# Output projection in block order 2, 0, 1, and the first feed-forward product begun with 20 direct tiles, in a hybrid diffusion layer on one core

## The chip, the cores and the metric

The kernel runs on one core of one Trainium2 chip. The metric is the device time of one launch in microseconds (us). A core has TensorE (PE in the profile; its weight loads are listed apart as PEld), VectorE (DVE), ScalarE (ACT), GpSimd (POOL) and SyncE (SP), which here issues nearly all DMA transfers. Each engine works through its own instructions in a fixed order, and an instruction whose operands are not ready holds up all that stand behind it on that engine.

## What is computed

One inference step of a one-layer backbone: 1024 sample tokens and 128 prompt tokens with 1024 features each. What the change touches is the end of the layer, from `merged` on; all of it is fp32.

```
merged = gates[..., :D] * (y_a @ w_proj_a) + gates[..., D:] * (y_b @ w_proj_b)
x = layer_norm(DN_ALPHA * x + gate1 * (merged @ w_out), ln1_g, ln1_b)     # 1024 x 1024
h = x * (1.0 + scale2) + shift2
f = jnp.square(jax.nn.relu(h @ w_ff1)) @ w_ff2                            # 1024 -> 4096 -> 1024
x = layer_norm(DN_ALPHA * x + gate2 * f, ln2_g, ln2_b)
```

Ahead of this stand the adaLN modulation, an input projection, a bidirectional state-space mixer and a gating unit.

## The kernel before

**Tokens and products.** The 1152 tokens are 9 chunks of 128 (chunks 0 to 7 sample, chunk 8 prompt), which make three blocks of 384 tokens: block 0 is chunks 0 to 2, block 1 chunks 3 to 5, block 2 chunks 6 to 8. An fp32 product is made as three fp32r matmuls on operands split in a high and a low part (`mm3`, L89 to L92: hi by hi, hi by lo, lo by hi). `split` (L80) makes the parts: ACT copies the raw tile to hi (L81), then DVE or POOL subtracts, lo = raw - hi (L86).

**Weights.** They come as tiles of 128x1024 (512 KB) through `take`, `more_raw` and `more_split` (L120 to L157): the load is issued on the SP queue (L126) into one of two `w_raw` buffers, and ACT and DVE split it into one of two `w_hi` and two `w_lo` buffers. So a tile can be split only when the tile two places ahead of it has been used up by PE, and loaded only when the tile two ahead has been split (and, in the first feed-forward product, summed).

**Order.** The program is written in one order; the framework's scheduler simulates it and fixes the order of instructions on each engine. `order()` (L113) adds a dependence by hand that carries no wait of its own.

**Output projection** (L876 to L923). For blocks 0, 1, 2 in turn: two halves of 512 output features (`tm_half`, L176), each of four weight tiles; a tile gives 18 matmuls of 512 columns. `ev_o` (L893) evicts the three chunks: DVE multiplies by the gate (L898) and adds the residual (L899). In the second half each chunk goes on at once: DVE statistics and 13 small operations for 1/sqrt by an integer guess and three Newton steps (`ln_stats`), ACT normalises (L904), a DMA stores the chunk to NX, PE transposes it (8 transposes, L912, into two small PSUM buffers), and ACT scales and shifts the result (L916) into `h2f0` or `h2f1` (blocks 0 and 1, fp32) or, for block 2, back in place and then split into `h2h` and `h2l`.

**Operands of the first feed-forward product (FF1)** (`combos`, L862). Blocks 0 and 1 share a Strassen-like scheme on quarters `q11, q21, q12, q22` of their activations: four subtractions of 128x1536 elements (L869 to L872) and seven operands (x11, x21, x22, xt4, xt2, xt3, xt1), each an ACT copy and a DVE subtraction of 128x1536. x11 and x21 are made after block 0, all the rest after block 1.

**FF1** (L978 to L1019). The 32 weight tiles go in 16 pairs. A pair makes seven half products for blocks 0 and 1 (12 matmuls of 384 columns each; four of them with sums of weight quarters, `S`, made by `sums`, L933) and two direct products for block 2 (24 matmuls each): 132 matmuls. `next_pair` takes the next tile after each direct product. Pair 0 has its direct products at the end, because block 2's `h2h` is made last; by hand the transposes of block 2 stand after pair 0's half products (L1008 to L1010). `keep` (L957) makes relu squared (ACT Relu and a DVE square for direct products, L960 and L961; two DVE operations otherwise) and stores it to HID. The second feed-forward product (FF2) follows, reading HID block by block from block 0 on.

Of the kernel before, what the change touches and what calls it, by code (L numbers as in the profile page):

```python
# [12 lines left out]
I32 = mybir.dt.int32  # L13
# [22 lines left out]
def tile_trunk(ctx: ExitStack, tc: tile.TileContext, I, O):  # L36
# [67 lines left out]
    FF0 = len(wsrc)  # L104
    wsrc += [("ff1", I["w_ff1"][i]) for i in range(FT)]
# [26 lines left out]
    def more_split(n):  # L132
        while state["split"] < min(n, len(wsrc)):
# [8 lines left out]
            for cs in cuts_of(i):  # L142
                split(raw[:, cs], hi[:, cs], lo[:, cs], lo_eng["eng"](i))
# [19 lines left out]
    def fm_block(pm, w, act, b, evict):  # L163
# [12 lines left out]
    def tm_half(pm, kind, act_b, evict, early=None):  # L176
        pss = [pm.tile([P, 512], F32, name="mm_ps", tag="mm") for _ in range(3)]
        for kp in range(4):
# [3 lines left out]
            for tt in range(3):  # L182
                for kk in range(2):
# [4 lines left out]
                        k == 0, k == KT - 1)  # L188
# [632 lines left out]
    for ft in range(KT):  # L821
# [12 lines left out]
        add_pos(ft)  # L834
# [20 lines left out]
    X, h_first = {}, {}  # L855

    def operand(name, src):
        t = blk.tile([P, 2, 4, TB], F32R, name=f"x{name}", tag="blk", bufs=NBLK)
        split(src, t[:, 0], t[:, 1], V)
        X[name] = (t[:, 0], t[:, 1])  # L860

    def combos(b):  # L862
        q11, q21, q12, q22 = quad[0, 0], quad[1, 0], quad[0, 1], quad[1, 1]
        if b == 0:
            operand("11", q11)
            operand("21", q21)
            return
        operand("22", q22)
        V.tensor_tensor(q11, q12, q11, op=SUB)  # L869
        V.tensor_tensor(q12, q22, q12, op=SUB)  # L870
        V.tensor_tensor(q22, q22, q11, op=SUB)
        V.tensor_tensor(q21, q22, q21, op=SUB)  # L872
        for name, q in (("t4", q21), ("t2", q22), ("t3", q12), ("t1", q11)):
            operand(name, q)

    for b in range(NB):  # L876
        if b == 2:
            h2b = [blk2.tile([P, KT, TB], F32R, name=f"h2{n}", tag="blk", bufs=NBLK2) for n in ("h", "l")]
        xr = []
        if b == 2:  # L880
            xr2 = blk2.tile([P, 3, D], F32, name="xr2", tag="blk", bufs=NBLK2)

        def load_xr():
            loads = [dma(out=g1[b], in_=GROW[0, b].partition_broadcast(P))] if b < 2 else []
            for c in range(3 * b, 3 * b + 3):
                r = tO.tile([P, D], F32, name="xr", tag="xr", bufs=3) if b < 2 else xr2[:, c % 3, :]
# [5 lines left out]
        for half in range(2):  # L892
            def ev_o(tt, ps):  # L893
                c = 3 * b + tt
                v = 0 if c < NL else 1
                hs = slice(half * 512, (half + 1) * 512)
                t = tO.tile([P, 512], F32, name="ot", tag="ot", bufs=1)
                V.tensor_tensor(t, ps, g1[v][:, hs], op=MUL)  # L898
# [3 lines left out]
                r = xr[tt]  # L902
                mv = ln_stats([r[:, 0:512], r[:, 512:1024]], tO)
                A.activation(r, r, AF.Identity, bias=mv[:, 2:3], scale=mv[:, 1:2])  # L904
                dma(out=NX[c], in_=r)
                for hf in range(2):
                    tp = pxB.tile([P, 4, P], F32, name="h2_ps", tag="aux")
                    ts = slice(tt * P, (tt + 1) * P)
                    ht = r.rearrange("p (k f) -> p k f", f=P)[:, 4 * hf:4 * hf + 4, :] if b == 2 else quad[hf, b][:, :, ts]
                    for a in range(4):  # L910
                        k = hf * 4 + a
                        ins = T.transpose(tp[:, a, :], r[:, k * P:(k + 1) * P], ident)  # L912
                        h_first.setdefault((c, hf), ins)
# [13 lines left out]
    NP = FT // 2  # L927
    S_HOME = [blk if p % 2 else blk2 for p in range(NP - 2)] + [blk, blk2]
    low, high = slice(0, 512), slice(512, D)

    def sums(p):
        r0, r1 = raw_of.pop(FF0 + 2 * p), raw_of.pop(FF0 + 2 * p + 1)
        pl = S_HOME[p]  # L933
        if p == 0:
            ops = [tO.tile([P, 2, 512], F32R, name="S", tag="xr", bufs=3) for _ in range(3)]
        else:
# [306 lines left out]
```

## Time and profile before

| | us |
|---|---|
| median of 3 runs | 1965.96 (1963.28 to 1967.21) |
| profiled execution | 1966.76 |
| its span, first to last instruction | 1965.0 |

| engine | busy us | share of the span |
|---|---|---|
| PE | 1882.0 | 96% |
| DVE | 1244.1 | 63% |
| ACT | 714.0 | 36% |
| POOL | 315.9 | 16% |

A page of the profile gives busy times for the span as a whole; the stretches that the change touches are read from windows, from the waits of PE and from the instructions in order of time. The output projection runs from about 1044 to 1150 us, FF1 from 1150 to 1558 us.

### The profile page before, as it was taken

What the parts mean: (1) busy time and instruction counts of PE and PEld (TensorE: products, weight loads), DVE (VectorE), ACT (ScalarE), POOL (GpSimd) and SP (SyncE); (2) the same over time, 40 slices, a digit from 0 to 9 for tenths busy, and PEclk for the clock granted to TensorE, in tenths of its full rate; (3) what the DMA queues carried; (4) which work ended last, traced back from release to release, by engine and by line L of the source; (5) the groups of instructions that cost most, each with busy time, mean ns of one, the idle gap of its engine ahead of it and who ended that gap; (6) DMA issues with size and microseconds to landing.
All of it is one profiled execution on the core that took longest, in us unless ns stands there. A gap on an engine that the chain in (4) does not pass through costs nothing.

```text
span 1965.0 us, 27909 instructions
## 1 busy us (share of the span) xinstructions
PE 1882.0 (96%) x10555; PEld 1721.4 (88%) x10555; DVE 1244.1 (63%) x2252; ACT 714.0 (36%) x1233; POOL 315.9 (16%) x254
## 2 busy tenths in 40 slices
PE   7999999899999999999999976999999999999998
PEld 4999998787898889999998766999999988878887
DVE  4756857999698353444455785666665555764855
ACT  4443424555413332333332554222222243433431
POOL 0332102333224530155220000000000000000001
PEclk9999999999999999999999987999999999999999
DMA  9145645455575331188545532333334775465551
GB/s 343 57 137 168 203 147 158 135 145 153 191 238 159 125 108 44 33 262 298 152 139 166 179 133 87 118 97 101 98 97 128 269 249 176 171 210 179 174 182 53
DMA packets 139879, 307.58 MB, mean 157 GB/s; under 512 B 14880, under 2 KB 78048, under 8 KB 138592
## 3 DMA queue, kind: packets, MB, share of 16 engines
q1 hardware_dynamic: 139744, 305.80, 47.4%
q8 instruction: 83, 1.36, 0.3%
q14 instruction: 52, 0.43, 0.1%
HBM read 244.23 MB, written 61.51 MB: 156 GB/s over the span
## 4 chain that ended last, share of the span: by engine, by line
PE 77%; DVE 11%; DMA 6%; issue 3%; ACT 2%; POOL 1%; SPq 1%; POOLq 0%; ACTq 0%; DVEq 0%
PE mm_ps L90 18%; PE mm_ps L91 18%; PE mm_ps L92 18%; PE ff_ps L92 6%; PE ff_ps L90 6%; PE ff_ps L91 6%; DVE Fb L584 2%; DVE cbD L587 1%; DVE w_lo L86 1%; DMA w<-in_w_ff_dram 1%; PE s_ps L737 1%; DMA Bb<-FB 1%; PE st_ps L526 1%; DMA xa<-NX 1%; PE y_ps L604 1%
## 5 line engine op out<-in xcount | busy, mean ns | idle before, releaser
L90 PE MATMUL mm_ps<-hTh,w_hi 128*128 128x384 f32 x1032 | 354.7, 347 | 0.8 <-ACT gt L623 0.8
L92 PE MATMUL mm_ps<-hTh,w_lo 128*128 128x384 f32 x1032 | 350.2, 339 | 1.2 <-DVE w_lo L86 1.2
L91 PE MATMUL mm_ps<-hTl,w_hi 128*128 128x384 f32 x1032 | 349.9, 339 | 0.0
L81 ACT ACTIVATE w_hi<-w_raw 128x1024 fp32r<-128x1024 f32 (+1 forms) x143 | 147.7, 1034 | 269.2 <-PE mm_ps L91 101.3
L86 DVE TENSOR_TENSOR w_lo<-w_raw,w_hi 128x1024 fp32r<-128x1024 f32 (+2 forms) x109 | 131.1, 1205 | 165.2 <-ACT w_hi L81 164.6
L90 PE MATMUL ff_ps<-w,hid 128*128 128x512 f32 (+1 forms) x552 | 210.0, 381 | 1.2 <-ACT hid L81 1.2
L91 PE MATMUL ff_ps<-w,hid 128*128 128x512 f32 (+1 forms) x552 | 209.6, 381 | 0.0
L90 PEld LDWEIGHTS mm_ps<-hTh,w_hi 128*128 128x128 f32 x1032 | 195.0, 190 | 11.7 <-issue 7.3
L91 PEld LDWEIGHTS mm_ps<-hTl,w_hi 128*128 128x128 f32 x1032 | 194.4, 188 | 8.9 <-issue 8.3
L92 PEld LDWEIGHTS mm_ps<-hTh,w_lo 128*128 128x128 f32 x1032 | 194.2, 188 | 5.6 <-issue 4.1
L92 PE MATMUL ff_ps<-w,hid 128*128 128x512 f32 (+1 forms) x552 | 170.9, 381 | 1.2 <-DVE hid L86 1.2
L1102 POOL TENSOR_TENSOR xa<-xa,row_lg 128x512 f32<-128x512 f32 (+1 forms) x11 | 15.2, 1396 | 905.2 <-PE ff_ps L92 675.7
L86 DVE TENSOR_TENSOR w<-w,w 128x1024 fp32r<-128x1024 f32 x96 | 117.2, 1222 | 57.9 <-ACT w L81 40.0
L90 PEld LDWEIGHTS ff_ps<-w,hid 128*128 128x128 f32 x552 | 103.8, 188 | 22.8 <-ACT hid L81 2.7
L92 PEld LDWEIGHTS ff_ps<-w,hid 128*128 128x128 f32 x552 | 103.3, 188 | 21.7 <-DVE hid L86 1.7
L91 PEld LDWEIGHTS ff_ps<-w,hid 128*128 128x128 f32 x552 | 103.8, 188 | 19.8
L81 ACT ACTIVATE w<-w 128x1024 fp32r<-128x1024 f32 x96 | 99.3, 1051 | 48.2 <-DMA w<-in_w_ff_dram 43.2
L81 ACT ACTIVATE hid<-hraw 128x384 fp32r<-128x384 f32 x88 | 45.9, 525 | 178.3 <-PE ff_ps L92 172.4
L86 DVE TENSOR_TENSOR hid<-hraw,hid 128x384 fp32r<-128x384 f32 x88 | 49.7, 567 | 82.0 <-ACT hid L81 82.0
L86 POOL TENSOR_TENSOR w_lo<-w_raw,w_hi 128x1024 fp32r<-128x1024 f32 x34 | 84.2, 2476 | 91.9 <-ACT w_hi L81 91.9
L90 PE MATMUL mm_ps<-h2h,w_hi 128*128 128x384 f32 x256 | 86.6, 339 | 3.2 <-ACT h2h L81 3.2
L81 ACT ACTIVATE S<-sum 128x512 fp32r<-128x512 f32 x64 | 39.8, 634 | 129.6 <-DVE sum L943 129.6
(304 smaller groups left out, 4255.2 us busy)
## 6 DMA issues: line engine op xcount, KB each, us to landing
w<-in_w_ff_dram SPq DMA_DIRECT2D x96, 512.0 KB, 5.2
HID<-sq SPq DMA_DIRECT2D x96, 192.0 KB, 2.2
hraw<-HID SPq DMA_DIRECT2D x96, 192.0 KB, 2.8
w_raw<-in_w_ff_dram SPq DMA_DIRECT2D x32, 512.0 KB, 4.0
w_raw<-in_w_v_dram SPq DMA_DIRECT2D x24, 512.0 KB, 3.6
w_raw<-in_w_out_dram SPq DMA_DIRECT2D x24, 512.0 KB, 3.7
Fb<-FB SPq DMA_DIRECT2D x36, 256.0 KB, 4.3
Bb<-FB SPq DMA_DIRECT2D x36, 256.0 KB, 5.1
```

The lines of the kernel that those rows point to most:

```text
L81: A.activation(hi, raw, AF.Copy)
L86: ins = eng.tensor_tensor(lo, raw, hi, op=SUB)
L90: T.matmul(ps, s[0], m[0], start=first, stop=False)
L91: T.matmul(ps, s[0], m[1], start=False, stop=False)
L92: return T.matmul(ps, s[1], m[0], start=False, stop=last)
L526: ins = T.matmul(st, Bk[:, c, g * P:(g + 1) * P], xws[g].rearrange("p h e -> p (h e)"), start=True, stop=True)
L584: V.scalar_tensor_tensor(Fb[:, i, :], Bb[:, i, :], QT[:, c, 3, h:h + 1], Fb[:, i, :], op0=SUB, op1=MIN)
L587: V.scalar_tensor_tensor(cbD[:, i, :], cbL[:, g, :], QT[:, c, 0, h:h + 1], cbD[:, i, :], op0=MUL, op1=ADD)
L604: ins = T.matmul(yp[64 * i:64 * i + 64, q, :], lhs[:, l0 + 64 * j:l0 + 64 * j + 64], rhs[:, j, :], start=n == 0, stop=n == len(terms) - 1)
L737: ins = T.matmul(sps[:, cc, :], Vh[b][:, cc, g * P:(g + 1) * P], WsT[:, g, :], start=True, stop=True)
L1102: mul.tensor_tensor(r[:, s], r[:, s], rows["lg"][:, s], op=MUL)
```

## The change

In the output projection the blocks come in the order 2, 0, 1 (`SEQ`). The layer norm's small operations are made once for the three chunks of a block (`ln_rows`, 128x3 elements) and no longer chunk by chunk. The transposes of a block are put by hand ahead of the first matmuls of the next block's second half (`after` in `tm_half`); those of block 1, which is now last, between the direct products 3 to 6 of FF1. Both gate rows `g1` are loaded with the first block. FF1 begins with 20 direct products for block 2 (tiles 0 to 19). Over those from the sixth on, eleven `tasks` are written one by one: the seven operands and the four subtractions. Then the 16 pairs follow in the order 0, 10, 1, 11, ..., 5, 15, 6, 7, 8, 9; pairs 0 to 9 have seven half products alone (84 matmuls), pairs 10 to 15 keep their two direct products (132). Tiles 0 to 19 are therefore loaded twice, and of ten of them only the upper half is split the second time (`upper`). All squares are made on ACT (Relu, then Square). `S` lies in `blk2` alone, `h2h` and `h2l` in `blk`.

```diff
-    wsrc += [("ff1", I["w_ff1"][i]) for i in range(FT)]
+    ND = 10
+    W_PAIRS = [p for q in range(FT // 2 - ND) for p in (q, ND + q)] + list(range(FT // 2 - ND, ND))
+    wsrc += [("ff1", I["w_ff1"][i]) for i in range(2 * ND)]
+    FF1 = len(wsrc)
+    wsrc += [("ff1", I["w_ff1"][2 * p + j]) for p in W_PAIRS for j in range(2)]
+    upper = {FF1 + 2 * q + 1 for q, p in enumerate(W_PAIRS) if p < ND}
...
-            for cs in cuts_of(i):
+            for cs in [slice(512, D)] if i in upper else cuts_of(i):
...
-                        k == 0, k == KT - 1)
+                        k == 0, k == KT - 1, [after[tt]] if after and k == 0 else ())
...
-        add_pos(ft)
+        add_pos((ft + 6) % KT)
...
-    for b in range(NB):
+    SEQ = (2, 0, 1)
+    for n, b in enumerate(SEQ):
...
-            loads = [dma(out=g1[b], in_=GROW[0, b].partition_broadcast(P))] if b < 2 else []
+            loads = [dma(out=g1[v], in_=GROW[0, v].partition_broadcast(P)) for v in range(2)] if n == 0 else []
...
-                mv = ln_stats([r[:, 0:512], r[:, 512:1024]], tO)
-                A.activation(r, r, AF.Identity, bias=mv[:, 2:3], scale=mv[:, 1:2])
+                V.bn_aggr(mv[:, tt, 0:2], st)
+                if tt < 2:
+                    return
+                ln_rows(mv, 3)
+                for j in range(3):
+                    second(j)
...
-            tm_half(pmB, "out", mp[b], ev_o, load_xr if half == 0 else None)
-        if b < 2:
-            combos(b)
+            tm_half(pmB, "out", mp[b], ev_o, load_xr if half == 0 else None,
+                    [h_last[3 * SEQ[n - 1] + j] for j in range(3)] if n and half else None)
...
+    tasks = deque([lambda: operand("11", q11), lambda: operand("21", q21),
+                   lambda: V.tensor_tensor(q11, q12, q11, op=SUB), lambda: operand("22", q22),
+                   lambda: V.tensor_tensor(q12, q22, q12, op=SUB), lambda: V.tensor_tensor(q22, q22, q11, op=SUB),
+                   lambda: V.tensor_tensor(q21, q22, q21, op=SUB), lambda: operand("t4", q21),
+                   lambda: operand("t2", q22), lambda: operand("t3", q12), lambda: operand("t1", q11)])
...
-        if y is None:
-            A.activation(t, x, AF.Relu)
-            V.tensor_tensor(t, t, t, op=MUL)
-        else:
+        if y is not None:
             V.tensor_tensor(t, x, y, op=op)
-            V.scalar_tensor_tensor(t, t, 0.0, t, op0=MAX, op1=MUL)
+            x = t
+        A.activation(t, x, AF.Relu)
+        A.activation(t, t, AF.Square)
...
+    spare = ["k1", "u2", "u3"]
+    for i in range(2 * ND):
+        done = direct(temp(spare[i % 3]), i, take("ff1"), [h_last[i - 1]] if 4 <= i < 7 else ())
+        if 3 <= i < 6:
+            order(h_first[i], done)
+        if i >= 5 and tasks:
+            tasks.popleft()()
...
-    for p in range(NP):
+    for q, p in enumerate(W_PAIRS):
...
-        if p:
-            direct(p, ft, f0)
-            next_pair(p + 1, 0)
+        if p >= ND:
+            direct(sq(), ft, f0)
+        next_pair(q + 1, 0)
```

What the scheduler makes of it is shown at three places. PE at the start of FF1, before: behind the half products of pair 0 (x22 by the last sum `S4`) stand the transposes of block 2's three chunks, and then the first direct product (`h2h`).

```order
L91 MATMUL mm_ps_10780<-x22_10286,S4_10666 128x384
L92 MATMUL mm_ps_10780<-x22_10286,S4_10666 128x384
L912 MATMUL h2_ps_10543<-ident_77,xr2_10307 128x128 x4
L912 MATMUL h2_ps_10554<-ident_77,xr2_10307 128x128 x4
...
L912 MATMUL h2_ps_10648<-ident_77,xr2_10307 128x128 x4
L90 MATMUL mm_ps_10797<-h2h_10305,w_hi_10494 128x384
L90 MATMUL mm_ps_10832<-h2h_10305,w_hi_10659 128x384
```

After, on PE at the same place, a direct product of block 2 follows the last matmul of the output projection, and the transposes of block 1's first chunk come four direct products later:

```order
L94 MATMUL mm_ps_10351<-w_hi_10400,ml1_8620 128x512
L90 MATMUL mm_ps_10561<-h2h_9594,w_hi_10424 128x384
L93 MATMUL mm_ps_10561<-h2l_9595,w_hi_10424 128x384
L94 MATMUL mm_ps_10561<-h2h_9594,w_lo_10425 128x384
...
L94 MATMUL mm_ps_10666<-h2h_9594,w_lo_10626 128x384
L924 MATMUL h2_ps_10489<-ident_77,xr_10244 128x128 x4
L924 MATMUL h2_ps_10498<-ident_77,xr_10244 128x128 x4
L90 MATMUL mm_ps_10701<-h2h_9594,w_hi_10660 128x384
```

The transposes of the last block no longer stand in one run with PE's next product behind them.

DVE at the making of the activation sums, before (the first rows; `h2f0` and `h2f1` hold blocks 0 and 1, `g1` the gates): they stand between the evictions of block 2, the splits of pair 0's weights and its sums.

```order
L899 SCALAR_TENSOR_TENSOR xr2_10307<-xr2_10307,ot_10416 128x512
L86 TENSOR_TENSOR w_lo_10471<-w_raw_10450,w_hi_10470 128x1024
L869 TENSOR_TENSOR h2f0_9592<-h2f1_9593,h2f0_9592 128x1536
L943 TENSOR_TENSOR sum_10667<-w_raw_10498 128x512
L943 TENSOR_TENSOR sum_10668<-w_raw_10474,w_raw_10498 128x512
L86 TENSOR_TENSOR w_lo_10495<-w_raw_10474,w_hi_10494 128x1024
L898 TENSOR_TENSOR ot_10518<-mm_ps_10419,g1_0_9583 128x512
L870 TENSOR_TENSOR h2f1_9593<-h2f1_9593 128x1536
L86 TENSOR_TENSOR x22_10286<-h2f1_9593,x22_10286 128x1536
```

After, on DVE, they stand between the weight splits of the direct products; `w_lo_10807` belongs to the ninth of them (direct 8, counted from 0), `w_lo_10917` to direct 11:

```order
L86 TENSOR_TENSOR w_lo_10769<-w_raw_10734,w_hi_10768 128x1024
L952 TENSOR_TENSOR h2f0_9592<-h2f1_9593,h2f0_9592 128x1536
L953 TENSOR_TENSOR h2f1_9593<-h2f1_9593 128x1536
L86 TENSOR_TENSOR x22_10876<-h2f1_9593,x22_10876 128x1536
L86 TENSOR_TENSOR w_lo_10807<-w_raw_10772,w_hi_10806 128x1024
...
L86 TENSOR_TENSOR w_lo_10881<-w_raw_10846,w_hi_10880 128x1024
L86 TENSOR_TENSOR xt4_11022<-h2f0_9592,xt4_11022 128x1536
L86 TENSOR_TENSOR xt2_11060<-h2f1_9593,xt2_11060 128x1536
L86 TENSOR_TENSOR xt3_11098<-h2f1_9593,xt3_11098 128x1536
L86 TENSOR_TENSOR xt1_11136<-h2f0_9592,xt1_11136 128x1536
L86 TENSOR_TENSOR w_lo_10917<-w_raw_10884,w_hi_10916 128x1024
```

Written one to a direct product, they have been scheduled in two clusters, ahead of the splits of direct 8 and of direct 11.

ACT at the same four operands, before (`k1` is the eviction of pair 0's first half product):

```order
L81 ACTIVATE w_hi_10659<-w_raw_10498 128x1024
L987 ACTIVATE k1_10696<-mm_ps_10683 128x384
L81 ACTIVATE S_10663<-sum_10667 128x512
L81 ACTIVATE xt4_10293<-h2f0_9592 128x1536
L81 ACTIVATE xt2_10296<-h2f1_9593 128x1536
```

After, on ACT, the four copies stand between Relu (L983) and Square (L984) of direct 8's result `u3_10841`, and the hi part of direct 11's weights behind them:

```order
L81 ACTIVATE w_hi_10880<-w_raw_10846 128x1024
L983 ACTIVATE u3_10841<-mm_ps_10848 128x384
L81 ACTIVATE xt4_11022<-h2f0_9592 128x1536
L81 ACTIVATE xt2_11060<-h2f1_9593 128x1536
L81 ACTIVATE xt3_11098<-h2f1_9593 128x1536
L81 ACTIVATE xt1_11136<-h2f0_9592 128x1536
L984 ACTIVATE u3_10841<-u3_10841 128x384
L81 ACTIVATE w_hi_10916<-w_raw_10884 128x1024
L983 ACTIVATE k1_10879<-mm_ps_10886 128x384
```

The cluster moved from between pair 0's half products to between the direct products of block 2.

## Rows read from the trace of the kernel before

**Rows 1.** PE's waits, 1040 to 1215 us: total, times, longest (us).
```profile
PE mm_ps L90 <- ACT xt L81: 12.1, 3, 10.7
PE h_ps L912 <- ACT xr L904: 6.3, 1, 6.3
PE h_ps L912 <- ACT xr L916: 5.7, 4, 3.8
PE mm_ps L90 <- ACT h2h L81: 3.2, 1, 3.2
PE mm_ps L91 <- DVE w_lo L86: 2.8, 1, 2.8
```

**Rows 2.** Windows: us, PE busy, PEld, DVE, ACT, POOL, PEclk, DMA share, GB/s.
```profile
1160.00:1210.00 50.00, 27.03 (x102) 23.29 (x103) 34.10 (x86) 25.10 (x45) 0.00 (x0) 0.61 0.20 73
...
1300.00:1400.00 100.00, 100.00 (x579) 100.00 (x578) 61.72 (x104) 24.54 (x38) 0.00 (x0) 1.00 0.31 99
```

**Rows 3.** PE over time, start of FF1 to FF2: start, us, line, operation, [idle before].
```profile
1150.16 0.33 PE L90 MATMUL mm_ps<-x,w_hi 128*128 128x384 f32 x1
...
1165.83 0.69 PE L90 MATMUL mm_ps<-xt,w_hi 128*128 128x384 f32 x1 [10.71 <-ACT xt L81]
...
1170.26 0.52 PE L92 MATMUL mm_ps<-xt,w_lo 128*128 128x384 f32 x1
...
1175.65 0.33 PE L92 MATMUL mm_ps<-xt,S 128*128 128x384 f32 x1
...
1204.30 1.01 PE L90 MATMUL mm_ps<-h2h,w_hi 128*128 128x384 f32 x2 [3.23 <-ACT h2h L81]
...
1558.48 0.39 PE L90 MATMUL ff_ps<-w,hid 128*128 128x512 f32 x1
```

**Rows 4.** PE over time, a stall in block 2's output projection.
```profile
1119.35 0.50 PE L91 MATMUL mm_ps<-w_lo,mh 128*128 128x512 f32 x1 [2.75 <-DVE w_lo L86]
1119.69 0.40 PE L92 MATMUL mm_ps<-w_hi,ml 128*128 128x512 f32 x1
```

**Rows 5.** DVE over time: block 0's first eviction, and ahead of that stall.
```profile
1074.59 0.68 DVE L898 TENSOR_TENSOR ot<-mm_ps,g 128x512 f32<-128x512 f32 x1
...
1113.55 1.75 DVE L86 TENSOR_TENSOR x<-h2f,x 128x1536 fp32r<-128x1536 f32 x1
...
1116.41 1.75 DVE L86 TENSOR_TENSOR x<-h2f,x 128x1536 fp32r<-128x1536 f32 x1
1118.08 1.22 DVE L86 TENSOR_TENSOR w_lo<-w_raw,w_hi 128x1024 fp32r<-128x1024 f32 x1
```

**Rows 6.** ACT over time in the output projection: weight splits, normalising, evictions, operands.
```profile
1051.95 1.06 ACT L81 ACTIVATE w_hi<-w_raw 128x1024 fp32r<-128x1024 f32 x1 [3.02 <-PE mm_ps L92]
1057.36 1.06 ACT L81 ACTIVATE w_hi<-w_raw 128x1024 fp32r<-128x1024 f32 x1 [4.34 <-DMA w_raw<-in_w_out_dram]
...
1087.81 1.24 ACT L904 ACTIVATE xr<-xr,ln_mv 128x1024 f32<-128x1024 f32 x1 [2.15 <-DVE ln_mv L213]
...
1100.21 2.91 ACT L916 ACTIVATE h2f<-h_ps,H,S 128x128 f32<-128x128 f32 x8 [1.42 <-PE h_ps L912]
...
1110.32 2.90 ACT L81 ACTIVATE x<-h2f 128x1536 fp32r<-128x1536 f32 x2
```

**Rows 7.** Window around the late weight tile (columns as in rows 2).
```profile
1051.00:1056.00 5.00, 5.00 (x24) 4.14 (x23) 1.23 (x1) 1.06 (x1) 0.00 (x0) 1.00 1.02 401
```

**Rows 8.** PE over time: one chunk's eight transposes at full clock.
```profile
1092.56 1.04 PE L912 MATMUL h_ps<-ident,xr 128*128 128x128 f32 x8
```

**Rows 9.** Groups by line and shape, 1210 to 1550 us: busy us, mean ns, idle before.
```profile
L86 DVE TENSOR_TENSOR w_lo<-w_raw,w_hi 128x1024 fp32r<-128x1024 f32 x30 | 36.8, 1226 | 94.5 <-ACT w_hi L81 94.5
...
L961 DVE TENSOR_TENSOR sq<-sq 128x384 f32<-128x384 f32 x31 | 17.1, 552 | 0.0
L960 ACT ACTIVATE sq<-mm_ps 128x384 f32<-128x384 f32 x31 | 14.6, 472 | 0.0
```

**Rows 10.** The page's DMA issues: count, KB each, us to landing.
```profile
w_raw<-in_w_ff_dram SPq DMA_DIRECT2D x32, 512.0 KB, 4.0
```

More of the change, by code (lines that the diff above doesn't have):

```diff
@@ L87, in split, with mm3 @@
         return ins
-    def mm3(ps, s, m, first, last):
-        T.matmul(ps, s[0], m[0], start=first, stop=False)
+    def mm3(ps, s, m, first, last, after=()):
+        ins = T.matmul(ps, s[0], m[0], start=first, stop=False)
+        for a in after:
+            order(ins, a)
         T.matmul(ps, s[0], m[1], start=False, stop=False)
@@ L854, in tile_trunk @@
     quad = {(r, b): h2f[b][:, 4 * r:4 * r + 4, :] for r in range(2) for b in range(2)}
[L855 to L874, printed above, removed]
@@ L876, in tile_trunk, with ln_rows @@
-    for b in range(NB):
-        if b == 2:
-            h2b = [blk2.tile([P, KT, TB], F32R, name=f"h2{n}", tag="blk", bufs=NBLK2) for n in ("h", "l")]
+    h2b = [block(blk, F32R, f"h2{n}", NBLK) for n in ("h", "l")]
+    X, h_first, h_last = {}, {}, {}
+    def ln_rows(mv, n):
+        x = mv[:, :, 1]
+        V.tensor_scalar(x, x, EPS, None, op0=ADD)
+        y = tO.tile([P, n], F32, name="ln_y", tag="ln_y", bufs=2)
+        t = tO.tile([P, n], F32, name="ln_t", tag="ln_t", bufs=2)
+        V.tensor_scalar(y.bitcast(I32), x.bitcast(I32), 1, None, op0=ALU.logical_shift_right)
+        V.tensor_scalar(y.bitcast(I32), y.bitcast(I32), -1, 0x5F3759DF, op0=MUL, op1=ADD)
+        for it in range(3):
+            V.tensor_tensor(t, y, x, op=MUL)
+            V.tensor_tensor(t, t, y, op=MUL)
+            V.tensor_scalar(t, t, -0.5, 1.5, op0=MUL, op1=ADD)
+            V.tensor_tensor(x if it == 2 else y, y, t, op=MUL)
+        V.scalar_tensor_tensor(mv[:, :, 2], mv[:, :, 0], -1.0, x, op0=MUL, op1=MUL)
@@ L901, in ev_o, with second @@
                     return
-                r = xr[tt]
-                mv = ln_stats([r[:, 0:512], r[:, 512:1024]], tO)
-                A.activation(r, r, AF.Identity, bias=mv[:, 2:3], scale=mv[:, 1:2])
+                st = tO.tile([P, 2, 6], F32, name="ln_st", tag="ln_st", bufs=2)
+                for i in range(2):
+                    V.bn_stats(st[:, i, :], xr[tt][:, i * 512:(i + 1) * 512])
+                V.bn_aggr(mv[:, tt, 0:2], st)
[4 more added lines that the diff above has]
+                    second(j)
+            def second(j):
+                c = 3 * b + j
+                v = 0 if c < NL else 1
+                r = xr[j]
+                A.activation(r, r, AF.Identity, bias=mv[:, j, 2:3], scale=mv[:, j, 1:2])
                 dma(out=NX[c], in_=r)
@@ L984, in tile_trunk @@
         ft = 2 * p
[L985 removed]
         k1, u2, u3 = temp("k1"), temp("u2"), temp("u3")
+        p1 = half_product(f0, "11")
         A.activation(k1, p1, AF.Copy)
[L988 to L997 removed]
+        p2 = half_product(f0, "21", high)
+        keep(sq(), ft, 0, p2, k1)
+        if p >= ND:
+            direct(sq(), ft, f0)
+        next_pair(q + 1, 0)
+        p4 = half_product(f1, "t4", high)
+        if p >= ND:
+            direct(sq(), ft + 1, f1)
+        next_pair(q + 1, 1)
+        p6 = half_product(s2, "t2")
         V.tensor_tensor(u2, p6, k1, op=ADD)
[L999 removed]
+        p7 = half_product(s3, "t3")
         V.tensor_tensor(u3, p7, u2, op=ADD)
[L1001 to L1003 removed]
+        keep(sq(), ft + 1, 0, u3, p4, SUB)
+        p5 = half_product(s1, "t1")
+        keep(sq(), ft + 1, 1, p5, u3)
         V.tensor_tensor(u2, p5, u2, op=ADD)
[L1005 to L1018 removed]
+        p3 = half_product(s4, "22")
+        keep(sq(), ft, 1, p3, u2)
     stV.close()
```

94 lines of the change are left out of this document (36 added, 58 removed).

## The prediction

> **What bounds the kernel now.** I read the waits of PE around the end of the output projection first, then the windows, then PE, DVE and ACT in order of time. In the windows of FF1 from 1210 us on, PE is busy without a break: 100.00 of 100 us, 579 matmuls, granted clock 1.00, so one matmul of 384 columns comes every 100 / 579 = 0.173 us [rows 2]. There is nothing to gain there. The start of FF1 is different. Between 1160 and 1210 us PE is busy 27.03 of 50 us, at a granted clock of 0.61 on average [rows 2], and PE's waits name the reasons in the order of the work [rows 1]: 12.1 us for operands xt on ACT (10.7 in one piece), 6.3 for the normalising of block 2, 5.7 for the evictions that free its two transpose buffers, 3.2 for h2h. Over time [rows 3]: PE stops ahead of 1165.83 because the four operands wait for the DVE subtractions; it starts again at the lower of its two clock levels (1.2 against 2.4 GHz; 17 matmuls from 1170.26 to 1175.65, 0.317 us each), and the same follows the wait that ends at 1204.30. A stall of 2.75 us at 1119.35 has another cause: two operand subtractions (DVE, 1.75 us each) stand ahead of the weights' lo part [rows 4, 5]. After that one the next matmul comes 0.34 us later and runs 0.40 us, near the full rate [rows 4]: a stall of this length did not take the clock down, one of 10.71 us did.
>
> **What the change removes.** FF1 lasts from 1150.16 to 1558.48 us [rows 3], 408.3 us. Its matmuls are 16 x 132 = 2112, before and after. At 0.173 us they take 365.4. Of the other 42.9 us, the 24 transposes of the last block are work that stays in this stretch: three times 1.04 [rows 8] = 3.1. So 39.8 us are waits and slow clock. All of them come from one thing: FF1's first pair needs sums over blocks 0 and 1, and its direct products need block 2, both of which are made at that moment. After the change, the first 20 tiles' direct products need only block 2, which was finished a whole block earlier, and take 20 x 24 x 0.173 = 83 us; the normalising of block 1 and the operands are made meanwhile. The two operands no longer stand together ahead of one weight split, so the 2.75 us of the present stall go as well; what one of them costs at its new place is in (c). Removed: 39.8 + 2.75 = 42.6 us.
>
> **What it adds, on the path.** (a) *The second gate row.* It is loaded with the first block, 512 KB more ahead of that block's next weight tile. That tile is already the late one: its hi part starts at 1057.36, 5.41 us after the one at 1051.95, where a tile's 18 matmuls of 512 columns take 18 x 0.173 x 512 / 384 = 4.15, and it waits for its DMA [rows 6], while the queues move 401 GB/s at a share of 1.02 [rows 7]. PE is still busy throughout [rows 7], but little can be left over. 524 KB at 401 GB/s is 1.3 us; bounds 0 (it finds room) and 2; I take 1.2.
>
> (b, c) *Transposes inside the next block's second half.* For the blocks 2 and 0 they now stand by hand ahead of the first products of the three chunks, and each chunk's eight evictions (2.91 us [rows 6]) stand on ACT ahead of a weight tile's hi part (1.06), which DVE's lo part (1.23 [rows 9]) follows: 5.2 us in a row where a tile lasts 4.15. With block 2, copies to h2h stand among them; with block 0, the operand x11, one half of the 2.90 us of two [rows 6], and its DVE part of 1.75 [rows 5]. In the present order the same row of work cost PE nothing at 1100.21, so the bounds of each are 0 and three times 1.1; since more is packed in, I take the upper end less a little, 3 us for each of the two halves, 6 in all.
>
> (d) *The two clusters in the direct products.* A direct product lasts 24 x 0.173 = 4.16 us. Block 1's last chunk is transposed behind direct 5; its evictions end about 1.04 + 2.91 = 3.95 us into direct 6. Only then can DVE make two subtractions and x22's lo part, which start 1.67 us apart [rows 5], and behind them stands direct 8's weight lo part, ready 3.95 + 5.0 + 1.2 = 10.15 us after direct 6 began; direct 8 wants it at 8.5. That is a wait of 1.65. Ahead of direct 11 stand four operands: after direct 8's Relu four ACT copies of 1.4, and four DVE subtractions of 1.67, the first of which can start 2.9 us into direct 9; direct 11's lo part is ready at 2.9 + 6.7 + 1.2 = 10.8 against 8.5, a wait of 2.3, less some 0.4 since the matmuls with hi alone are put ahead. With 0.25 us for the two transpose buffers, (d) is 1.65 + 1.9 + 0.25 = 3.8; bounds 0 (the subtractions find gaps that I don't see) and 8 (each cluster costs twice as much).
>
> (e) *What lies beside other work.* Ten more splits of whole tiles and ten of upper halves (ACT 1.06, DVE 1.23 for a whole one), and 20 more loads of 512 KB. In a direct product ACT has 1.06 + 2 x 0.47 [rows 6, 9], DVE 1.23, of 4.16 us. In a pair of half products alone (84 x 0.173 = 14.5 us) DVE has two splits, four sums with their lo parts and the combinations, some 11 us by the same rows, ACT less. So neither is the bound; I cost them at 0, and if the cover failed a pair would be late by what DVE exceeds 14.5, on ten pairs at most 10 us in all. The 96 squares taken off DVE (552 ns each [rows 9]) cost and gain nothing where PE waits for no one. In the clusters of (d) they would stand ahead of the late splits.
>
> The Trainium skill (ScalarE: Activation LUTs, Rules for kernel authors) speaks against this last part: Relu, maxima and products belong on VectorE rather than ScalarE. The rows say otherwise for this form: ACT's Relu over 128x384 took 472 ns, DVE's square 552 ns [rows 9]. Going by the page, the squares would stay on DVE, each of the two waits of (d) would be up to 0.55 us longer, and the time 1936; going by the rows it is 1935.
>
> **The sum.** 42.6 removed; 1.2 + 6 + 3.8 = 11.0 added. The profiled execution took 1966.76 us, so 1966.76 - 31.6 = 1935.2; the median of the runs is 0.8 lower, which I leave out. Forecast 1935, with its own range from 1928 to 1942 by the bounds that can fall together.
>
> **Rivals.** *No new waits.* Each of (a) to (d) comes out near its lower end: 1966.8 - 42.6 = 1924. For it speaks that the chain of evictions and splits cost PE nothing at 1100.21; against it the stall at 1119.35, which is the same thing as the two clusters [rows 4, 5].
>
> *The old waits come back in another place.* Block 1's normalising has to be ready when its transposes' turn comes, four direct products (16.6 us) after FF1 begins. Block 0's first normalising began 13.2 us after its first eviction (1074.59 to 1087.81 [rows 5, 6]) and takes 1.24, and now it waits for all three chunks' statistics; some 2 us are left over. If they aren't there, PE waits behind direct 3 for the normalising and then for the buffers, at most as now 6.3 + 5.7 [rows 1], and restarts at the low clock, which costs 17 x (0.317 - 0.173) = 2.4 [rows 3]: 1935.2 + 14.4 = 1950. The change would do half of what it says.
>
> *Slower than before: direct products that aren't fed.* The place is the two raw buffers during the first 20 tiles. A buffer's round is its load (4.0 us [rows 10]), then ACT 1.06 and DVE 1.23, 6.3 us, and two direct products give it 8.3. It decides when the landing grows past 6.0 us; beyond that each tile is late by half of the excess, and to eat the 31.6 us over 20 tiles takes 3.2 us of excess, a landing of 9.2. At 10 us it would be (10 + 2.3 - 8.3) / 2 x 20 = 40 us, 1975. Against it: the output projection's tiles are as short (4.15 us), and one tile was late there, while 2 MB were loaded beside it [rows 6, 7].
>
> **How the numbers follow.** Forecast 0.56, no new waits 0.20, old waits 0.17, unfed 0.04; the remaining 0.03 is a mixture of the last two that ends within 0.2% (about 4 us, what a measurement of this kernel can tell from no change). Faster 0.93, same 0.03, slower 0.04. The range for 8 in 10 is 1922 to 1950: from no new waits, less 2 for the estimate of the rate, up to the waits that come back.
>
> **What would show it.** In the changed profile: FF1's first matmul is a direct product within a microsecond of the last one of the output projection; from there to FF2's first matmul it takes some 372 us (365.4 + 3.1 + 3.8) and the granted clock stays 1.00; PE's waits name w_lo or w_hi at directs 8 and 11 with 1 to 3 us; the output projection from first to last matmul is some 4 us longer than now (7.2 added, 2.75 gone), with waits for w_lo, w_hi or the transpose buffers in the second halves of blocks 0 and 1; the pairs show none. Wrong would be: a wait for the normalising behind direct 3, waits for w_raw's DMA in the directs, or a granted clock under 1 in them; and waits in the short pairs for S or w_lo, which I cost at nothing.

## The result and the profile after

The changed kernel takes 1937.0 us (median of four runs, 1936.3 to 1941.1) against 1965.3 before: ratio 0.986, 95% interval 0.9843 to 0.9878. The forecast was 1935. The profiled execution has a span of 1935.2 us.

The time is best followed in four stretches: up to the first matmul of the output projection, from there to the first matmul of the first feed-forward product (FF1), from there to the first of the second (FF2), and to the end. All four borders are rows of PE in order of time.

| us | ahead | output projection | FF1 | FF2 and end | span |
|---|---|---|---|---|---|
| before | 1043.6 | 106.6 | 408.3 | 406.5 | 1965.0 |
| after | 1040.4 | 114.8 | 373.3 | 406.6 | 1935.2 |
| difference | -3.1 | +8.2 | -35.0 | +0.1 | -29.8 |

The first column can't be told from scatter. Ahead of the output projection the change moves only the order of `add_pos`; the eleven variants below, which all have that and alter nothing more there, lie between 1038.8 and 1044.4. So in the trace the change gives 26.6 us, from the output projection on, and that sum (span less the first column; before 921.4, after 894.8) is what the traces of the experiments are compared by.

The waits of PE from the output projection to the end of FF1, in the changed kernel (us in total, times, longest), answer to rows 1:

```profile
PE mm_ps L90 <- ACT w_hi L81: 6.6, 5, 2.1
PE mm_ps L93 <- DVE w_lo L86: 1.6, 3, 1.0
PE mm_ps L94 <- DVE w_lo L86: 0.5, 1, 0.5
PE h_ps L924 <- ACT h2f L929: 0.3, 1, 0.3
PE h_ps L924 <- ACT xr L929: 0.3, 1, 0.3
```

No wait for an operand xt, for the normalising or for h2h is left (L929 is the eviction of a transposed chunk); 8.7 of the 9.3 us that remain are for weight splits. Where they lie, PE in order of time (start, us, line, operation, idle before; L90, L93 and L94 are the three matmuls of a product):

```profile
1058.44 0.96 PE L90 MATMUL mm_ps<-w_hi,mh 128*128 128x512 f32 x3 [1.48 <-ACT w_hi L81]
1059.70 0.50 PE L93 MATMUL mm_ps<-w_lo,mh 128*128 128x512 f32 x1 [0.30 <-DVE w_lo L86]
...
1060.42 0.63 PE L90 MATMUL mm_ps<-w_hi,mh 128*128 128x512 f32 x1
...
1106.73 0.96 PE L90 MATMUL mm_ps<-w_hi,mh 128*128 128x512 f32 x3 [1.35 <-ACT w_hi L81]
...
1145.67 0.96 PE L90 MATMUL mm_ps<-w_hi,mh 128*128 128x512 f32 x3 [2.14 <-ACT w_hi L81]
1147.65 0.50 PE L93 MATMUL mm_ps<-w_lo,mh 128*128 128x512 f32 x1 [1.02 <-DVE w_lo L86]
1147.99 0.39 PE L94 MATMUL mm_ps<-w_hi,ml 128*128 128x512 f32 x1
...
1155.27 0.33 PE L90 MATMUL mm_ps<-h2h,w_hi 128*128 128x384 f32 x1
...
1205.09 0.44 PE L90 MATMUL mm_ps<-h2h,w_hi 128*128 128x384 f32 x1 [0.88 <-ACT w_hi L81]
...
1206.42 0.44 PE L90 MATMUL mm_ps<-h2h,w_hi 128*128 128x384 f32 x1 [0.70 <-ACT w_hi L81]
...
1207.55 0.69 PE L94 MATMUL mm_ps<-h2h,w_lo 128*128 128x384 f32 x1 [0.49 <-DVE w_lo L86]
...
1528.55 0.39 PE L90 MATMUL ff_ps<-w,hid 128*128 128x512 f32 x1
```

There are four places: the first tile of block 2's second half (1058), the second half of block 0 (1107), that of block 1 (1146), and directs 11 and 12 (1205). Behind the first and the last, matmuls of 0.63 and 0.69 us show the lower clock.

A stop costs more than the wait that is listed for it: the three matmuls at 1145.67 took 1.98 us to the next one at 1147.65, where the full pace (0.227 us each) makes 0.68, so 1.30 were lost where the list has 1.02. Counted like this, from start to start and with the slow matmuls, the changed kernel lost 3.9 us at 1058, 3.0 in block 0's second half, 4.2 in block 1's, and 4.2 at directs 11 and 12: 15.3 in all.

In windows (us, PE busy, PEld, DVE, ACT, POOL, PEclk, DMA share, GB/s) the stretch of rows 2 that had a granted clock of 0.61 now has 0.97, and the pairs are as full as they were:

```profile
1160.00:1210.00 50.00, 47.92 (x274) 46.51 (x273) 32.77 (x41) 38.37 (x65) 0.00 (x0) 0.97 0.54 178
1230.00:1330.00 100.00, 100.00 (x579) 100.00 (x578) 62.57 (x95) 54.41 (x98) 0.00 (x0) 1.00 0.40 131
```

What makes directs 11 and 12 late stands on ACT in order of time: four copies as one piece between the weight splits.

```profile
1196.75 1.06 ACT L81 ACTIVATE w_hi<-w_raw 128x1024 fp32r<-128x1024 f32 x1 [3.44 <-DMA w_raw<-in_w_ff_dram]
1197.71 0.48 ACT L983 ACTIVATE u<-mm_ps 128x384 f32<-128x384 f32 x1
1198.08 5.61 ACT L81 ACTIVATE xt<-h2f 128x1536 fp32r<-128x1536 f32 x4
1203.59 0.51 ACT L984 ACTIVATE u<-u 128x384 f32<-128x384 f32 x1
1204.00 1.04 ACT L81 ACTIVATE w_hi<-w_raw 128x1024 fp32r<-128x1024 f32 x1
```

### The profile page after: what moved, and what is told of

The parts are those of the page before. It is cut to its first block, busy times and chain, and to the rows that moved or that the text cites. A ratio compares the mean times of both kernels' runs of the same rounds, so it can differ in the third digit from the quotient of the medians.

```text
span 1935.2 us, 27993 instructions
## 1 busy us (share of the span) xinstructions
PE 1876.0 (97%) x10555; PEld 1715.9 (89%) x10555; DVE 1214.2 (63%) x2107; ACT 802.2 (41%) x1413; POOL 317.1 (16%) x254
## 4 chain that ended last, share of the span: by engine, by line
PE 76%; DVE 11%; DMA 6%; ACT 3%; issue 3%; POOL 1%; SPq 0%; POOLq 0%; ACTq 0%; DVEq 0%
PE mm_ps L93 18%; PE mm_ps L94 18%; PE mm_ps L90 17%; PE ff_ps L94 6%; PE ff_ps L90 6%; PE ff_ps L93 6%; DVE Fb L590 1%; DVE w_lo L86 1%; PE y_ps L610 1%; DVE cbD L593 1%; DVE X L671 1%; DVE crow L250 1%; PE s_ps L743 1%; DMA ada_b<-in_w_ada_dram 1%; PE st_ps L532 1%
## 5 line engine op out<-in xcount | busy, mean ns | idle before, releaser
L90 PE MATMUL mm_ps<-hTh,w_hi 128*128 128x384 f32 x1032 | 354.0, 347 | 0.7 <-ACT gt L629 0.7
L94 PE MATMUL mm_ps<-hTh,w_lo 128*128 128x384 f32 x1032 | 350.1, 339 | 0.0
L93 PE MATMUL mm_ps<-hTl,w_hi 128*128 128x384 f32 x1032 | 349.9, 339 | 0.0
L81 ACT ACTIVATE w_hi<-w_raw 128x1024 fp32r<-128x1024 f32 (+2 forms) x163 | 164.5, 1011 | 263.1 <-PE mm_ps L93 136.0
L86 DVE TENSOR_TENSOR w_lo<-w_raw,w_hi 128x1024 fp32r<-128x1024 f32 (+2 forms) x129 | 150.0, 1165 | 147.8 <-ACT w_hi L81 147.2
L90 PE MATMUL ff_ps<-w,hid 128*128 128x512 f32 (+1 forms) x552 | 209.8, 381 | 1.8 <-ACT hid L81 1.8
L93 PE MATMUL ff_ps<-w,hid 128*128 128x512 f32 (+1 forms) x552 | 209.6, 380 | 0.0
L90 PEld LDWEIGHTS mm_ps<-hTh,w_hi 128*128 128x128 f32 x1032 | 194.3, 189 | 11.0 <-issue 7.3
L93 PEld LDWEIGHTS mm_ps<-hTl,w_hi 128*128 128x128 f32 x1032 | 194.4, 188 | 8.9 <-issue 7.0
L94 PEld LDWEIGHTS mm_ps<-hTh,w_lo 128*128 128x128 f32 x1032 | 194.2, 188 | 4.3 <-issue 4.3
L94 PE MATMUL ff_ps<-w,hid 128*128 128x512 f32 (+1 forms) x552 | 171.1, 380 | 1.0 <-DVE hid L86 1.0
L1121 POOL TENSOR_TENSOR xa<-xa,row_lg 128x512 f32<-128x512 f32 (+1 forms) x11 | 15.3, 1404 | 877.8 <-ACT xa L1120 877.8
L90 PEld LDWEIGHTS ff_ps<-w,hid 128*128 128x128 f32 x552 | 103.8, 188 | 22.6 <-ACT hid L81 2.8
L94 PEld LDWEIGHTS ff_ps<-w,hid 128*128 128x128 f32 x552 | 103.3, 188 | 21.3 <-DVE hid L86 1.4
L93 PEld LDWEIGHTS ff_ps<-w,hid 128*128 128x128 f32 x552 | 103.8, 188 | 19.8
L90 PE MATMUL mm_ps<-h2h,w_hi 128*128 128x384 f32 x256 | 86.6, 338 | 1.6 <-ACT w_hi L81 1.6
L94 PE MATMUL mm_ps<-h2h,w_lo 128*128 128x384 f32 x256 | 86.3, 338 | 0.5 <-DVE w_lo L86 0.5
```

Source lines behind the costliest of these rows:

```text
L81: A.activation(hi, raw, AF.Copy)
L86: ins = eng.tensor_tensor(lo, raw, hi, op=SUB)
L90: ins = T.matmul(ps, s[0], m[0], start=first, stop=False)
```

## The experiments

The theory: FF1's gain comes from work that stands beside the 20 directs (the normalising and transposes of block 1, and the sums), and the losses are weight splits that come late for three separate reasons: one late load, and two rows of work ahead of the splits on ACT and DVE. The rivals: the gain comes from the block order, the batched layer norm or the squares; the losses are a general lack of room on ACT, DVE or the queues. All variants start from the changed kernel.

**e10: the sums behind the directs.** Each part is also held behind the last weight split, as in e3 below.

```diff
-        if i >= 5 and tasks:
-            tasks.popleft()()
+        while i == 2 * ND - 1 and tasks:
+            made = tasks.popleft()()
...
```

> The operands and subtractions are all held back by hand to the end of the direct products (behind the split of the first pair's first tile), so that the directs cover the layer norm of block 1 and its transposes, but not the sums. Theory (what the directs hide is the waits that pair 0 had before the change: 10.7, 0.7, 0.7, 0.5 us and some 4 us of slow matmuls behind them, some 16 us): these come back ahead of pair 0, less the 4.2 us at 1205 us and some 2 us at 1146 that go: 1937 + 10 = 1947, between 1943 and 1955. Rival (the gain comes from the block order, the batched layer norm and the squares, and the place of the sums matters little): 1931 to 1938.

Measured: 1946.7 us (1943.8 to 1948.2). From the output projection on 901.6 us, FF1 385.7 against 373.3. PE's waits in FF1 are the old ones of rows 1, at the new place:

```profile
PE mm_ps L90 <- ACT xt L81: 12.6, 2, 11.9
PE mm_ps L93 <- DVE x L86: 0.6, 1, 0.6
```

So hiding the sums beside the directs is worth about what they cost ahead of pair 0. The normalising and its transposes, still covered here, do not come back as waits. Some 18 us against the kernel before remain without the sums' share; no run here tells the block order from the directs in them, since the directs need block 2 to be finished first.

**e3: the sums truly one to a direct.** Each operand's ACT copy and each DVE part is held behind the split of the weight tile last written (dependences on the same engine); in e2 only x11 and x21 are held.

```diff
...
-            tasks.popleft()()
+            made = tasks.popleft()()
+            if 1 <= 11 - len(tasks) <= 11:
+                hi, lo = made if type(made) is tuple else (None, made)
+                order(lo, state["w_lo"])
+                if hi is not None:
+                    order(hi, state["w_hi"])
```

> All eleven operands and subtractions are held back by hand, one behind the weight split of each direct from the fifth on, on ACT and on DVE, so that the clusters ahead of directs 8 and 11 are gone. Theory (the cluster of four costs the waits and the slow clock around 1205 us, about 4.2 us, and x11 and x21 those of 3.2 at 1146): 1937.0 - 7.4 = 1929.6 if nothing comes back, 1932 with half of x11's and x21's share back. Rival (ACT and DVE have too little room in the directs however it is spread): waits of 1 to 2 us at several directs, 1935 to 1940.

> The operands x11 and x21 are held back by hand to directs 5 and 6 (each behind the split of the next tile), where the program has them; in the changed kernel the scheduler puts them into the last half of the output projection. Theory (they are what makes the last weight tiles of the output projection late): the waits of 2.14 and 1.02 us at 1146 us go, 3.2 us. In directs 4 to 7 ACT then has 1.06 + 1.0 + 2.9 + 1.5 = 6.4 us for 4.16 at two tiles, so that up to 3 of it can come back there: 1934 to 1937, 1935 if half comes back. Rival (the weights are late there because of the evictions alone): no change, 1937.

Measured: e3 1929.3 us (1928.0 to 1932.8), ratio to before 0.9827 (0.9808 to 0.9845). FF1 takes 369.5 us, which is the 365.4 of its matmuls, the 3.1 of its transposes and 1 us; its only wait is

```profile
PE h_ps L925 <- ACT h2f L930: 0.4, 1, 0.4
```

and the window of the directs runs at full clock:

```profile
1152.00:1252.00 100.00, 99.56 (x584) 99.22 (x583) 63.95 (x79) 67.62 (x108) 0.00 (x0) 1.00 0.55 177
```

There was room enough on ACT and DVE (68 and 64 of 100 us busy); the cluster was the cost. e2 came out at 1937.7 (1933.3 to 1940.1); its trace, of the fastest of its runs, gives 892.7, 2.1 below the changed kernel. The pair of waits at 1146 shrank from 2.14 and 1.02 to 0.77 and 0.30, not to nothing, while FF1 became 2.3 longer behind the cluster that stayed. So x11 and x21 are only part of what stands ahead of the last tiles. In both traces the output projection is 4.6 us shorter, but only some 2.1 of that lies at 1146; the rest lies at 1058, which neither edit touches: the waits there are 0.24 and 0.28 in e2, 0.45 and 0.29 in e3, and the clock did not fall behind them.

**e8: the transposes of blocks 2 and 0 where the scheduler puts them.**

```diff
             tm_half(pmB, "out", mp[b], ev_o, load_xr if half == 0 else None,
-                    [h_last[3 * SEQ[n - 1] + j] for j in range(3)] if n and half else None)
+                    None)
```

> The transposes of blocks 2 and 0 are not put by hand ahead of the first products of the next block's second half; the scheduler places them. In its order each group of four or eight evictions has a weight split between, where the changed kernel has 24 and 20 evictions in a row around one or two. Theory (these groups make the next weight tile late): the waits at 1107 us (1.35 + 0.30) and about 1 us of those at 1146 go, but x11 and x21 now stand together ahead of the third direct product's split and cost 1 to 2 there: 1934 to 1937. Rival (the scheduler puts the transposes where PE would wait for their operands): waits for xr or h_ps, 1938 to 1942.

Measured: 1929.1 us (1927.6 to 1931.2), ratio 0.9827 (0.9812 to 0.9841), more than expected. The output projection takes 104.9 us against 114.8. From 1060 us to its end one wait is left:

```profile
PE mm_ps L93 <- DVE w_lo L86: 0.3, 1, 0.3
```

It belongs to the place at 1058. The hand-made order of the transposes caused all of the waits in the second halves of blocks 0 and 1. Of the 9.9 us, counted from start to start, 7.2 lie in these two halves; the other 2.7 lie at 1058, which this edit does not touch (waits of 0.54 and 0.29 here, and no slow matmuls). FF1 is 2.0 us longer (375.3): x11 and x21 now make the third direct's split late, as expected (a wait of 0.62 at 1156), and one of 0.66 for the transposes' buffers at 1171 comes to it.

**e1: the first block's loads in three pieces.**

```diff
...
-            loads = [dma(out=g1[v], in_=GROW[0, v].partition_broadcast(P)) for v in range(2)] if n == 0 else []
-            for c in range(3 * b, 3 * b + 3):
+            loads = [dma(out=g1[kp], in_=GROW[0, kp].partition_broadcast(P))] if n == 0 and kp < 2 else []
+            for c in [3 * b + kp] if n == 0 else range(3 * b, 3 * b + 3):
```

> The loads ahead of block 2 (two gate rows and three residual chunks, 2.5 MB, issued in one piece behind one weight tile in the changed kernel) are issued in three pieces behind three weight tiles. Theory (the second gate row makes a weight tile late): the waits of 1.48 and 0.30 us at 1058 us and the slow matmuls behind them (about 1.6 us) go, 1937.0 - 3.4 = 1933.6. Rival (the sum of the bytes in that stretch is what delays, wherever they are issued): another tile is late by as much, 1936 to 1938.

Measured: 1936.7 us (1935.6 to 1938.3), by the time of the launch no change. The trace says otherwise: the only wait between 1044 and 1100 us is

```profile
PE h_ps L926 <- ACT xr L931: 0.3, 1, 0.3
```

so the late tile is gone, and with it the 3.9 us of this place. The output projection is only 2.1 us shorter, because slow matmuls followed the unchanged waits of block 1's half (from 1148.74 on), where the changed kernel had none. From the output projection on the sum is 891.0, 3.8 less; the other 1.6 lies in FF1, which the edit does not touch: this time the clock did not fall behind directs 11 and 12. This execution began the output projection at 1044.4, the latest of all, which hides it in the total. The gain is shown for this place and trace, not for the launch.

**e4 and e12: squares on DVE, in the changed kernel and in the best one.**

```diff
-        if y is not None:
-            V.tensor_tensor(t, x, y, op=op)
-            x = t
-        A.activation(t, x, AF.Relu)
-        A.activation(t, t, AF.Square)
+        if y is None:
+            A.activation(t, x, AF.Relu)
+            V.tensor_tensor(t, t, t, op=MUL)
+        else:
+            V.tensor_tensor(t, x, y, op=op)
+            V.scalar_tensor_tensor(t, t, 0.0, t, op0=MAX, op1=MUL)
```

> Squares as before the change (DVE, ACT only Relu for direct products); all else as changed. Theory (neither engine holds up PE in the pairs, and the squares cost or gain nothing): 1937 to 1938, the waits around 1205 us up to 0.5 longer, none in the pairs. Rival (the squares' move is what gives DVE room in the pairs without direct products): DVE has four more operations of 0.55 in pairs of 14.5 us; waits for w_lo or S in ten pairs, 1942 to 1947.

> e9 with the squares on DVE as before the change. Theory (the 4 us that the squares on DVE cost in e4 came only through the cluster at 1205 us and through restarts at the low clock, and DVE has room everywhere else): the same as e9 within 2 us, 1920 to 1924. Rival (the squares on ACT are worth 4 us on their own, in the pairs and at the start of FF2): 1925 or more, with waits for w_lo or S in the pairs or a longer wait at the start of FF2.

Measured: e4 1941.4 us (1938.7 to 1941.9), 4 more than the changed kernel and more than the theory allowed; e12 1923.1 against e9's 1922.4 (below), no difference. In e4 there is no wait in the pairs; the waits at directs 11 and 12 became 1.28, 0.72 and 0.90 instead of 0.88, 0.70 and 0.49, and FF1 2.4 us longer, with some 16 slow matmuls behind them in place of 8. The output projection is 1.6 longer with the same waits, at a granted clock of 0.94 from 1095 to 1150 us where the changed kernel had 1.00; that has nothing to do with squares. FF2 is 2.1 longer, some 0.4 of it a longer wait at its start. With the clusters gone, e12 has no wait at all from the first matmul of the output projection to the end of FF1, and the difference is gone too. So the pairs have room for the squares on either engine; what they cost in e4 they cost at the clusters, as far as it is not scatter.

**e6 and e13: how many directs are needed.** e6 changes the changed kernel (`ND = 5`, ten directs), e13 the best one (`ND = 8`, 16 directs).

> Ten direct products ahead of the pairs in place of 20, and ten tiles loaded twice in place of 20 (pairs 0 to 4 without direct products, 5 to 15 with). The last operand is ready 51 us after the first direct product began in the changed kernel (1206.3 less 1155.3), ten directs with three times eight transposes last 45 us, and pair 0's sums and splits now stand between the operands on DVE. Theory (20 directs are more than needed, ten are too few): pair 0 waits 4 to 8 us in pieces, with 2.4 us of slow matmuls: 1944, between 1940 and 1949. Rival (pair 0's first products need only x11 and x21, which are ready, and hide the rest): 1934 to 1938.

> e9 with 16 direct products first in place of 20, four tiles fewer loaded twice, and pairs in the order 0, 8, 9, 1, 10, 11, 2, 12, 13, 3, 14, 15, 4 to 7. Theory (the cover is needed only until the last operand is made, one per direct from the fifth to the fifteenth): the same as e9 within 1.5 us, 1920 to 1923. Rival (16 are just too few, since x and xt end with the last direct and pair 0 needs its sums from the same engine): a wait of 2 to 5 us ahead of pair 0, 1924 to 1927.

Measured: e6 1938.2 us, but between 1934.5 and 1947.4; e13 1922.6 (1919.6 to 1927.9), the same as with 20. e6's profiled execution is its slowest run. Its waits in FF1 are two:

```profile
PE mm_ps L94 <- DVE w_lo L86: 2.5, 1, 2.5
PE mm_ps L90 <- ACT w_hi L81: 1.3, 1, 1.3
```

That is 3.8 us where 4 to 8 were expected, FF1 is 2.7 us longer than with 20 directs, and the median lies below the 1940 to 1949 expected. My expectation counted the operands as if pair 0 wanted them all at once; it wants them over 14.5 us, which I take to be the reason. Against the trace of the changed kernel this slowest execution loses 3.8 us ahead of the output projection (1044.3), 2.9 in it (117.7, with nearly the same waits, but low clock behind those at 1111 and 1153, where the changed kernel kept the full one), 2.7 in FF1 and 0.9 in FF2. Its faster siblings left no trace. Ten directs are nearly enough, 16 are enough; the exact need stays open within the scatter.

**e7: the layer norm chunk by chunk.**

```diff
-                if tt < 2:
-                    return
-                ln_rows(mv, 3)
-                for j in range(3):
-                    second(j)
+                ln_rows(mv[:, tt:tt + 1, :], 1)
+                second(tt)
```

> The layer norm's small operations chunk by chunk (three times 14 operations of 128x1 in place of 14 of 128x3), and each chunk normalised when its own are done; all else as changed. Theory (DVE has room in that stretch, and the turn of the transposes is set by hand): no change, 1936 to 1939. Rival (the batch is what lets the last block be normalised before direct 4): a wait for xr on PE behind direct 3 of 2 to 5 us, 1939 to 1945.

Measured: 1938.4 us (1936.0 to 1940.4). PE waits 1.87 us for xr at 1101 in block 0's half and not behind direct 3; its output projection is 3.4 us longer than the changed kernel's, its FF1 1.8 shorter. The batch is worth no more than the measurement can tell.

**e9: e1, e3 and e8 together.**

> Three of the edits together: the first block's loads in three pieces (e1), the operands and subtractions held to one per direct product (e3), and the transposes of blocks 2 and 0 left to the scheduler (e8). Theory (the new waits of the change have three separate causes, each of which one edit removes): from the first matmul of the output projection the changed kernel took 894.8 us to the end, e3 885.3, e8 886.2; e8's output projection less the 0.8 us at 1059 is 104.1, e3's FF1 369.5, FF2 405.6, together 879: 1937 - 16 = 1921, between 1919 and 1925. Rival (the slots in the directs are full, and what e8 spreads in the output projection collides with what e3 holds back): waits in directs 2 to 8 of 2 to 5 us, 1924 to 1929.

Measured: 1922.4 us (1920.4 to 1924.1), ratio to before 0.9786 (0.9773 to 0.98). From the output projection on 879.6, 15.2 below the changed kernel: that is what the four places cost there from start to start (15.3). The windows of the output projection and of FF1, and all of PE's waits in them:

```profile
1041.00:1144.00 103.00, 103.00 (x478) 85.38 (x478) 69.07 (x122) 50.43 (x80) 0.00 (x0) 1.00 0.61 207
1144.00:1513.00 369.00, 368.56 (x2137) 368.21 (x2135) 224.64 (x334) 208.30 (x365) 0.00 (x0) 1.00 0.46 151
```

```profile
PE h_ps L927 <- ACT h2f L932: 0.4, 1, 0.4
```

But for this wait, PE works without a break at full clock over 472 us. This version beats both kernels.

## Why the prediction came out right, point by point

**What is removed** (42.6 us): right. The 39.8 us of FF1 were waits and slow clock and nothing else: with the collisions gone (e3, e9) FF1 takes 369.5 us where the prediction's floor was 365.4 + 3.1, and e9 against the kernel before is 41.8 us from the output projection on. e10 shows for the sums' share that their place among the directs is what does it, and e7 and e12 that the batched norm and the squares are not. That the waits for the normalising, the buffers and h2h went because of the directs is read from the trace alone, which has none of them left. The 2.75 us of rows 4 did go.

**(a) The second gate row** (1.2 us): the place was right: PE's wait at 1058.44 is for this weight split, which its load released:

```profile
1057.33 1.06 ACT L81 ACTIVATE w_hi<-w_raw 128x1024 fp32r<-128x1024 f32 x1 [7.43 <-DMA w_raw<-in_w_out_dram]
```

That the loads issued in one piece are the cause, e1 shows; no run takes away the second row's 512 KB alone. The term cost 1.48 + 0.30 us of waits and 1.4 more, since seven matmuls from 1060.42 on came 0.427 us apart instead of 0.227. The prediction had no such term: from the one case in rows 4, 2.75 us at full clock, it gave short stalls no price in clock. The size is partly chance: in the seven variants that leave these loads as they are, the two waits add up to 0.5 to 2.5 us, and the clock fell in one of them (e6).

**(b, c) Transposes by hand** (6 us): 1.95 us of waits in block 0's half (1.35, 0.30, 0.30) and 3.47 in block 1's (2.14, 1.02, 0.31), 5.4 in all, and 7.2 from start to start. The cause was right for both, the transposes by hand and the evictions in a row on ACT that follow, and e8 shows how large the term is: all 7.2 go when the order is left free. x11 and x21 in block 1's half (e2) are part of it. The note in the prediction that the same work cost nothing at 1100.21 was the better guide to what could be had.

**(d) The clusters** (3.8 us): in sum right (2.07 us of waits, and 1.3 from 1207.55 to 1210.28, where eight matmuls took 2.73 us instead of 1.39; 4.2 from start to start), in its parts not. Direct 8 was to wait 1.65 us and lost 0.16: the first subtraction needs only half of the last chunk's evictions and started at 1184.96, before they ended, and the lo part was done at 1191.74, when direct 8 was at its third matmul, the first that needs it. DVE and PE in order of time:

```profile
1190.52 1.22 DVE L86 TENSOR_TENSOR w_lo<-w_raw,w_hi 128x1024 fp32r<-128x1024 f32 x1
...
1191.46 0.34 PE L93 MATMUL mm_ps<-h2l,w_hi 128*128 128x384 f32 x1
1191.79 0.44 PE L94 MATMUL mm_ps<-h2h,w_lo 128*128 128x384 f32 x1
```

Nearly the whole cost fell on directs 11 and 12.

**(e) What lies beside other work** (0): right for the pairs, which have no wait, and no wait of PE in the directs is put down to a load. But one weight split there was released by its load (1196.75, above). Direct 10's load was issued at 1191.77, as soon as direct 8's split was done, and landed 4.9 us later; its split began 1.0 us after direct 8 was used up (direct 9 begins at 1195.73). The four copies and direct 11's split stand behind it on ACT. So the first cluster, which made direct 8's split late, may have cost up to 1 us of the waits at directs 11 and 12 through this load; no run separates the two.

**The rivals.** The directs were fed (loads landed in 3.6 us, median, in this stretch), but for the one case in (e). The normalising of block 1 was ready in time: its first step started at 1169.14, the transposes behind direct 3 at 1171.94, without a wait:

```profile
1169.14 3.50 ACT L916 ACTIVATE xr<-xr,mv 128x1024 f32<-128x1024 f32 x3
...
1171.94 1.03 PE L924 MATMUL h_ps<-ident,xr 128*128 128x128 f32 x8
```

No new waits was not the outcome, but it was to be had: e9 stands below it by 1.6 us.

**The sum.** Predicted from the output projection on: -31.6. Measured there: -26.6. The 5 us are 3.8 in the output projection and 1 in FF1. What the change removes came out nearly as predicted (41.8 against 42.6); what it adds was priced too low, 11.0 against 15.3: the waits listed in the output projection are the 7.2 predicted, but each stop cost more than its wait, and behind the first one the clock fell. That the total came so close is in part luck: the first stretch of the profiled executions, 3.1 us apart, is within its scatter.

The Trainium skill (ScalarE: Activation LUTs, Rules for kernel authors) puts Relu and products on VectorE. Here ACT's Square took 523 ns and DVE's 552 over the same 128x384 fp32 elements, and e12 shows no difference in the time; the rule decides nothing where neither engine is waited for.

## What to carry to other kernels

Work that only delays the tensor engine because of where it stands is worth moving behind products that need none of it; how many such products are needed is read from the last operand's time and when each is first wanted. Look at the scheduled order before trusting the written one: eleven operations written one to a product were scheduled in clusters, and holding each behind its neighbour's split gave back 7.7 us of the launch, of which the trace shows some 5.9 at the places that the edit touches. An order forced by hand is worth taking away again as an experiment: here it cost 7.2 us where it stood. And compare traces place by place: the place at 1058 differed by up to 2.8 us between kernels that treat it alike.

## What the runs showed of the hardware

**The same wait, two clocks.** The waits of 2.14 and 1.02 us in block 1's half are the same in several executions. In the changed kernel the matmuls behind them run 0.39 us and 0.23 apart (1147.99, above). In e4 they come at the lower of the two levels:

```profile
1144.16 0.96 PE L90 MATMUL mm_ps<-w_hi,mh 128*128 128x512 f32 x3 [2.13 <-ACT w_hi L81]
1146.14 0.80 PE L93 MATMUL mm_ps<-w_lo,mh 128*128 128x512 f32 x1 [1.02 <-DVE w_lo L86]
1146.73 0.63 PE L94 MATMUL mm_ps<-w_hi,ml 128*128 128x512 f32 x1
...
1149.29 0.52 PE L90 MATMUL mm_ps<-w_hi,mh 128*128 128x512 f32 x1
```

So a wait's length alone does not tell whether the clock falls; a fall costs 1.3 to 2.4 us here. The runs of e6, where PE stops in several places, lie between 1934.5 and 1947.4, those of e9, where it hardly stops, between 1920.4 and 1924.1. That such falls are what makes the difference between runs of one kernel is not shown: only one execution of each has a trace, and the run with the lowest mean clock is the slowest in e6 (0.990) but the fastest in e9 (0.992).
